# Differential attention: low parts of the queries with zeros on the other 64 partitions

## Chip, cores and metric

The kernel runs on one core of one Trainium2 chip. Times are device microseconds of one execution of the whole program; a change is judged by the median of several executions.

## What is computed

The program is a model of two blocks with two layers each, on 512 tokens of width 1024 (and, in the first block, 256 context tokens). The change touches the differential attention of the first block's second layer alone. It has 8 heads; each has two halves of 64 features, with a softmax of its own each, and one value of 128 features.

```python
def attend(q, k, v):                      # q, k: [2 halves, batch, 8 heads, tokens, 64]
    s = jnp.einsum('cbhqd,cbhkd->cbhqk', q, k).astype(f32)
    p = jax.nn.softmax(s, axis=-1)
    a = p[0] - lam_val * p[1]
    return jnp.einsum('bhqk,bhkv->bhqv', a, v.astype(f32))
...
k_all = jnp.concatenate([kl, kc], axis=3)     # 512 + 256 keys
o_lat = attend over 4 blocks of 128 queries
o = _rmsnorm(o, subln_g) * (1.0 - lambda_init)
```

Queries and keys of the 512 latent tokens are turned by a rotary embedding (rope) first.

## The kernel before

Each product in full precision is made of products of split operands: a number is a high part and a low part, each with at most 12 significant bits, and TensorE adds high x high, low x high and high x low.

Heads are done in four pairs. `project(pr)` (line 1122) is a generator that projects the keys, queries and values of a pair in 12 steps. `ev_q` (line 1127) takes a query head out of PSUM: rope into a scratch tile `qraw` (with a second scratch tile `rot`), then the high part, then the low part. The tile `q` [128, 3, 512] holds three planes. Plane 0 and plane 1 (`cc`) have the high part of half `cc` twice, on its own 64 partitions and on the other 64. Plane 2 has the low parts of both halves, each on its own 64 partitions. `ev_k` (line 1138) does the same for a key head with the scratch `kraw`; its tile `kx` [128, 2, 768] has for half `cc` the high part on its own partitions and the low part on the other ones.

`attend` (line 1171) takes one head, in four blocks `t` of 128 queries. For each half and each 384 of the 768 keys there are two score products into one bank: plane `cc` of `q` against `kx[:, cc]` on all 128 rows (high x high and high x low at once), then plane 2 on the 64 rows of the half against the key's high part:

```python
self.mm(s[cc][:, f, 0:384], q[:, cc, t * P:(t + 1) * P], kx[:, cc, fs], stop=False)
self.mm(s[cc][:, f, 0:384], q[cp, 2, t * P:(t + 1) * P], kx[cp, cc, fs], start=False)
```

So a block has 8 score products and a head 32; the layer has 256. Then VectorE takes the maximum (`nm`, line 1186), ScalarE the exponential (line 1189), VectorE combines the two halves (line 1196), TensorE transposes the result in 4 + 2 pieces through the one bank `a` with a copy by ScalarE after each (line 1203), and multiplies it with the values into bank `o`. After the fourth block `head_norm_out` (line 1227) norms the head in a tile `ho`: a product on VectorE (1232), squares on ScalarE, a power on GpSimd, a second product on VectorE (1240), and four transposes into bank `a`.

The table `da_fill` says how many of the next pair's projection steps go between the blocks of a head: (2, 2, 2, 2, 0) for the first head of a pair and (2, 2, 0, 0, 0) for the second. The last pair has steps of the output projection in their place (`da_last`). A scheduler orders the instructions of each engine from this program when it is built; on the chip each engine takes its instructions in that order. Eight PSUM banks are shared: two for projections (`g`), one `a`, one `o`, two pairs of banks for scores (`s2`). Weights come through SP's DMA queue. `after` (in the first block's program) loads the gate row of the output projection into the tile that was `kraw`, for line 1250.

Of the kernel before, what the change touches and what calls it, by code (L numbers as in the profile page):

```python
# [40 lines left out]
class Kernel:  # L41
    # how many steps of independent work go into the gaps of a chain, ring sizes, scheduling priorities
# [25 lines left out]
    # ---------------------------------------------------------------- helpers  # L68
# [27 lines left out]
    def banks(self, **turns):  # L96
        """a tag takes the banks of these tags in turn (2: halves of s2)"""
        self.turns, self.rest = {k: itertools.cycle(v) for k, v in turns.items()}, None

    def psum(self, **nb):  # L100
        """(re)partition the 8 PSUM banks among tags"""
        if self.pb is not None:
            self.pb.release()
        self.nb = nb
        self.pb = self.pool("ps", 1, PSUM) if nb else None

    def setup(self):
# [17 lines left out]
        self.le = tri("le", -1, 1, ALU.is_ge)   # [p, f] = p <= f  # L125
        self.ge = tri("ge", 1, -1, ALU.is_ge)   # p >= f
        self.gt = tri("gt", 1, -1, ALU.is_gt)   # p > f
        self.lt = tri("lt", -1, 1, ALU.is_gt)   # p < f
# [5 lines left out]
    def open_w(self, raw, hi, unit, side):  # L134
        """rings of weight tiles: raw, high and low parts"""
        return unit, self.pool("wraw", raw, side=side), self.pool("whi", hi, side=side), self.pool("wlo", hi, side=side)
# [8 lines left out]
    def rsqrt(self, out, in_, mul, add, exponent=None):  # L145
        """out = (in_ * mul + add) ** -0.5 on GpSimd, tiny operands"""
# [11 lines left out]
    def exp_ln_tables(self):  # L158
        """the activation tables that hold both exp and ln, from here on"""
        self.tc.keep_in_program_order(self.nc.scalar.preload_act_table_set("natural_log_exp_and_others"))  # L160
# [8 lines left out]
    def rows_to_cols(self, rows, tag, pool=None):  # L169
        """rows: DRAM APs [r, 128] -> const tile [128, sum r], whose columns self.finish_cols() fills"""  # L170
# [18 lines left out]
    def split(self, hi, lo, src, hi_eng):  # L189
        """hi + lo = src exactly, each with at most 12 significant bits"""  # L190
# [3 lines left out]
    def weights(self, src, a, mul=None):  # L194
        """DRAM view [128, a, unit // a] (times mul) -> hi, lo tiles of that shape"""
# [11 lines left out]
    # weights stationary: feature-major result, 256 output features at a time  # L207
# [3 lines left out]
    def gemm_steps(self, w, c0, groups, evac, ncol=256):  # L211
        """groups: lists of segments; a segment is (hi(kt), lo(kt), n). evac(j, [psum per segment])"""
# [12 lines left out]
    def ws_tile(self, ps, wk, j, segs, kts=range(NK)):  # L225
        """128 output features of the segments"""
# [6 lines left out]
    def gemm_halves(self, parts, segs):  # L233
        """the same of several (weights, first column, evac), where the last tokens come late: all products of the
        first segment go ahead"""
# [11 lines left out]
    # tokens stationary: token-major result, 512 output features at a time  # L247
# [14 lines left out]
    def ts_pair_steps(self, wk, hh, hl, t, out):  # L262
        """token tiles t, t + 1, 256 output features each, in the halves of a bank"""
# [16 lines left out]
    # ---------------------------------------------------------------- modulation  # L280
    def ada_setup(self):
# [11 lines left out]
        # column v of s4: vector v; the four column tiles of the array take a k tile each  # L293
# [3 lines left out]
        # sel[r, v]: rows that add up to vector v: v of each column tile, and the bias in row 2; then without the bias  # L297
# [19 lines left out]
    def ada_block(self, l, n, row):  # L317
        """products with columns n * 512 .. of ada_w[l] into row [128, 512], to be summed by sel"""
# [13 lines left out]
    def ada_cols(self, l, sec):  # L332
        """section sec of layer l, feature-major: [128, 8, 2] (lat, ctx)"""
# [13 lines left out]
    def ada_bc_store(self, l, sec, dst):  # L347
        """section sec of layer l to DRAM rows dst [2, 1024] (lat, ctx), to be read back on all partitions"""
# [12 lines left out]
    def load_bc(self, pool, row, tag, n=D):  # L361
        """a DRAM row [n] on all partitions"""
# [4 lines left out]
    # ---------------------------------------------------------------- gated delta net (layer 0)  # L367
# [3 lines left out]
    def load_transposed(self, x_src, ctx_src, xp):  # L371
        """the rows of x and ctx, feature-major: 8 tiles [128, 768]"""
# [21 lines left out]
    def deltanet(self, xp, xT, scratch, zs, gts, later):  # L394
        """normed, gated head outputs before norm_g go to scratch; returns the transposed y"""
# [7 lines left out]
        # shift, scale and the first products, in halves of the features  # L403
# [37 lines left out]
        # decay and beta  # L441
# [52 lines left out]
        def conv_silu2(blk, dst, ps):  # L494
            """dst = 2 silu(conv(x))"""
# [16 lines left out]
        for grp in range(4):  # L512
# [7 lines left out]
            # independent work for the gaps of the chains  # L520
# [26 lines left out]
    def dn_gate(self, half, w, hh, hl, onep, zs):  # L547
        """2 silu(z) of two heads, token-major, to DRAM"""
# [11 lines left out]
    def dn_project(self, grp, w, segs, one, onep, conv_silu2, beta, eg, fill, first):  # L560
# [8 lines left out]
        def sums(src, tag):  # L569
            """sums of squares per token, of twice the value"""  # L570
# [3 lines left out]
            # as rows, two chunks per column tile of the array; then transposed  # L574
# [64 lines left out]
    def dn_tmp(self, one, shape):  # L639
        """one of a ring of 4 KB scratch tiles"""  # L640
# [8 lines left out]
    def dn_prepare(self, p, one, g):  # L649
        """inverses of both directions' triangular systems, and the q k products times the decays: their upper  # L650
        triangle is for direction 0, the lower one for direction 1"""
# [4 lines left out]
        for j, h in enumerate(heads):  # L656
            # decays between tokens j, i: a sum over an empty range in one of the two directions
# [34 lines left out]
    def dn_invert(self, Wt, one):  # L692
        """Wt[:, u] (unit triangular but for its diagonal; u < 12 upper, u >= 12 lower) -> its inverse, in place"""
# [7 lines left out]
        # [(b, i), u, j] -> [(b, u), i, j]: one matrix per partition  # L701
# [17 lines left out]
        # [0]: blocks of the inverse, [1]: their transposes; direction 0 was inverted transposed  # L719
# [8 lines left out]
        # 32 -> 64: source block row, target block row, per direction and pair  # L728
# [23 lines left out]
        # transposed 64-blocks: direction 0 in rows 0:64, direction 1 in rows 64:128  # L752
# [8 lines left out]
        # 64 -> 128  # L761
# [106 lines left out]
    def dn_store(self, p, O, one, scratch):  # L868
        """half the normed head outputs to DRAM"""
# [17 lines left out]
    # ---------------------------------------------------------------- shared pieces  # L887
    def dn_output(self, k, scratch, zs, yh, yl, yp, zp):
        """y = norm(o) * silu(z), transposed and split into yh, yl (norm_g applied on the way)"""
# [16 lines left out]
    def scaled_split(self, hi, lo, ps, scale):  # L906
        """hi + lo = ps * scale"""
# [39 lines left out]
    def proj_steps(self, w, xh, xl, k0, k1, tiles, evac, ncol=512):  # L947
        """token-major projection of k tiles k0 .. k1 of the transposed, split activations by w, in steps;
        evac(t, c0, psum[:, :ncol])"""
# [13 lines left out]
    def ln_stats(self, x, pool):  # L963
        """1 / std and mean per token"""
# [10 lines left out]
    def layernorm(self, x, pool):  # L975
        """x <- (x - mean) * rstd, per token"""
# [6 lines left out]
    def layernorm_affine(self, x, g, b, pool):  # L983
        """x <- (x - mean) * rstd * g + b, per token"""
# [10 lines left out]
    def transpose_split(self, xt, hh, hl, t0, t1, sc, sh, pool, tag="s"):  # L995
        """token tiles xt[t0:t1] -> feature-major hi / lo columns, times sc(k) plus sh(k) per feature"""
# [19 lines left out]
    def fold_cols(self, tag, g, b, sc, sh):  # L1016
        """LN gain and bias folded into the modulation: scale g (1 + sc), bias b (1 + sc) + sh; [128, 8, 2] each"""
# [18 lines left out]
    # gated FFN; gate/up feature-major, down token-major, in chunks of the hidden features  # L1036
    def ffn(self, ntok, emit_hidden, w_down, acc, sb, nring, sizes, add=False, before=None, final=None, mul=None,
            order=None):
        """emit_hidden(pair, hi tiles, lo tiles): two hidden feature tiles. acc[t] (+)= hidden @ w_down, in chunks of
        sizes, w_down times mul; before(): ahead of the last chunk, whose product goes to final(t, c0, psum)"""  # L1040
# [23 lines left out]
        # the down product runs behind the hidden features  # L1064
# [22 lines left out]
    # ---------------------------------------------------------------- differential attention (layer 1)  # L1087
# [1176 lines left out]
```

## Time and profile before

| | |
|---|---|
| median of 3 runs | 3865.22 us |
| lowest, highest | 3863.72, 3866.85 us |
| profiled execution, span of its instructions | 3858.7 us |
| TensorE busy | 3740.8 us, 97% |
| weight loads of TensorE busy | 3033.0 us, 79% |
| VectorE busy | 2343.5 us, 61% |
| ScalarE busy | 1541.7 us, 40% |
| GpSimd busy | 440.1 us, 11% |

The profile is one execution; its page gives the span from the first to the last instruction. In its rows PE is TensorE's matmuls and PEld its weight loads, DVE is VectorE, ACT ScalarE, POOL GpSimd, SP SyncE, and SPq the DMA queue that SP fills. `g<-wh,h3h` names tiles as out<-in: the first input of a matmul is the moving one, the second the stationary one. A matmul's length is its way through the array, so matmuls overlap, and the rate is read from start to start. "issue" is idle time in which the engine waited for nothing that the profile shows.

### The profile page before, as it was taken

To read this page: it belongs to the slowest core of one execution; us is meant where nothing else is said; L and a number is where in the kernel's file an instruction comes from. 1 tells how busy PE (TensorE), PEld (TensorE's weight loads), DVE (VectorE), ACT (ScalarE), POOL (GpSimd) and SP (SyncE) were. 2 spreads that over 40 slices of the span, in tenths; PEclk is the share of its full clock that TensorE was granted. 3 is DMA by queue.
4 is the path that set the end of the run, shared out by engine and by line. 5 is a ranking of instruction groups with operands and counts; after the bars stand their busy time and mean duration, and the time that the engine had idled before them with its cause. 6 is when DMAs were issued, how large, how long until landed. Compare 5 with 4: busy or idle time off the path is not lost.

```text
span 3858.7 us, 57682 instructions
## 1 busy us (share of the span) xinstructions
PE 3740.8 (97%) x23195; PEld 3033.0 (79%) x23195; DVE 2343.5 (61%) x3919; ACT 1541.7 (40%) x2836; POOL 440.1 (11%) x642
## 2 busy tenths in 40 slices
PE   8999999999999999998999999999999999999999
PEld 5675766888888877777888877788887888888887
DVE  3757655653333676677555656656666777556665
ACT  3444443332211244454222456544334655444332
POOL 3112211040000020003000102100000222100000
PEclk9999999999999999999999998999999999999999
DMA  4234234512122211113333213212332223223232
GB/s 166 77 96 132 88 118 126 175 61 66 56 65 66 69 59 33 34 50 91 98 97 91 86 55 106 65 60 88 99 96 86 72 67 106 87 66 93 91 95 82
DMA packets 248974, 329.47 MB, mean 85 GB/s; under 512 B 14408, under 2 KB 194988, under 8 KB 248705
## 3 DMA queue, kind: packets, MB, share of 16 engines
q1 hardware_dynamic: 248000, 325.40, 27.2%
q8 instruction: 182, 2.98, 0.3%
q14 instruction: 88, 0.71, 0.1%
q0 software_dynamic: 704, 0.37, 0.0%
HBM read 318.09 MB, written 7.63 MB: 84 GB/s over the span
## 4 chain that ended last, share of the span: by engine, by line
PE 83%; DVE 6%; ACT 4%; POOL 3%; issue 2%; DMA 1%; SPq 0%; ACTq 0%; POOLq 0%; DVEq 0%
PE g L163 41%; PE a L163 16%; PE o L163 13%; PE s L163 7%; PE i L163 2%; PE s L167 1%; PE a L167 1%; PE p L163 1%; DVE wl L204 1%; DMA araw<-in_ada_w_dram 1%; ACT wh L203 1%; ACT xr L1480 1%; ACT xr L1477 0%; DVE bst L968 0%; PE g L167 0%
## 5 line engine op out<-in xcount | busy, mean ns | idle before, releaser
L204 DVE TENSOR_TENSOR wl<-wr,wh 128x1024 fp32r<-128x1024 f32 (+1 forms) x508 | 587.6, 1164 | 435.8 <-ACT wh L203 420.8
L203 ACT CAST wh<-wr 128x1024 fp32r<-128x1024 f32 (+1 forms) x508 | 493.5, 981 | 783.6 <-PE o L163 373.1
L163 PE MATMUL g<-wh,fh 128*128 128x512 f32 x396 | 156.4, 395 | 0.0
L163 PE MATMUL g<-wh,fl 128*128 128x512 f32 x396 | 156.1, 395 | 0.0
L163 PE MATMUL g<-wl,fh 128*128 128x512 f32 x396 | 155.1, 392 | 0.0
L163 PE MATMUL g<-h2l,wh 128*128 128x512 f32 x352 | 138.0, 392 | 2.4 <-DVE h2l L1014 2.4
L163 PE MATMUL g<-h2h,wh 128*128 128x512 f32 x352 | 137.5, 392 | 0.0
L163 PE MATMUL g<-h2h,wl 128*128 128x512 f32 x352 | 137.1, 390 | 0.0
L163 PE MATMUL a<-araw,s 128*32 128x512 f32 x352 | 125.7, 617 | 6.2 <-DMA araw<-in_ada_w_dram 5.9
L163 PE MATMUL g<-hh,wh 128*128 128x512 f32 (+1 forms) x376 | 115.7, 363 | 1.7 <-ACT hh L421 1.5
L152 POOL TENSOR_SCALAR brs<-bmv 128x1 f32<-128x1 f32 x20 | 9.7, 484 | 932.1 <-DVE bmv L970 922.9
L163 PE MATMUL g<-hh,wl 128*128 128x512 f32 (+1 forms) x376 | 112.6, 358 | 3.5 <-DVE wl L204 3.5
L163 PE MATMUL g<-hl,wh 128*128 128x512 f32 (+1 forms) x376 | 114.0, 358 | 0.8 <-POOL hl L422 0.6
L1049 DVE TENSOR_TENSOR x<-g,x 128x512 f32<-128x512 f32 x120 | 82.5, 688 | 30.5 <-PE g L163 30.3
L163 PE MATMUL s<-k,q 128*128 128x384 f32 (+1 forms) x256 | 98.7, 440 | 0.0
L1186 DVE TENSOR_REDUCE nm<-s 128x1 f32<-128x768 f32 x64 | 61.1, 955 | 52.3 <-PE s L163 52.3
L163 PEld LDWEIGHTS g<-hh,wh 128*128 128x128 f32 x376 | 63.5, 193 | 35.5 <-issue 20.5
L163 PEld LDWEIGHTS g<-hl,wh 128*128 128x128 f32 x376 | 63.4, 192 | 32.6 <-issue 23.7
L163 PEld LDWEIGHTS g<-hh,wl 128*128 128x128 f32 x376 | 62.7, 192 | 32.4 <-issue 21.3
L163 PEld LDWEIGHTS g<-wh,fh 128*128 128x128 f32 x396 | 74.4, 188 | 17.4 <-ACT fh L2096 0.6
L1291 ACT CAST fh<-sg 128x768 fp32r<-128x768 f32 (+1 forms) x44 | 32.0, 726 | 138.9 <-DVE sg L1290 138.9
L163 PEld LDWEIGHTS g<-wl,fh 128*128 128x128 f32 x396 | 74.4, 188 | 16.6
(994 smaller groups left out, 11513.5 us busy)
## 6 DMA issues: line engine op xcount, KB each, us to landing
wr<-in_ffn_w_up_dram SPq DMA_DIRECT2D x132, 512.0 KB, 3.7
araw<-in_ada_w_dram SPq DMA_DIRECT2D x192, 256.0 KB, 3.1
wr<-in_ffn_w_down_dram SPq DMA_DIRECT2D x88, 512.0 KB, 3.7
wr<-in_ffn_w_gate_dram SPq DMA_DIRECT2D x44, 512.0 KB, 3.8
wr<-in_dn_w_in_dram SPq DMA_DIRECT2D x66, 256.0 KB, 2.8
wr<-in_xa_w_kv_dram SPq DMA_DIRECT2D x32, 512.0 KB, 3.9
wr<-in_hgrn_w_in_dram SPq DMA_DIRECT2D x32, 512.0 KB, 4.2
wr<-in_da_w_in_dram SPq DMA_DIRECT2D x24, 512.0 KB, 3.5
```

Of the source, the lines that this page charges most:

```text
L152: nc.gpsimd.tensor_scalar(out=out, in0=in_, scalar1=mul, scalar2=add, op0=MUL, op1=ADD)
L163: self.nc.tensor.matmul(out, lhsT=lhsT, rhs=rhs, start=start, stop=stop)
L167: self.nc.tensor.transpose(out, in_, self.ident[0:k, 0:k])
L203: nc.scalar.copy(hi, raw)
L204: nc.vector.tensor_tensor(out=lo, in0=raw, in1=hi.bitcast(F32), op=SUB)
L1049: nc.vector.tensor_tensor(out=a, in0=ps, in1=a, op=ADD)
L1186: nc.vector.tensor_reduce(out=nm, in_=s[cc][:, :, 0:384], axis=AX.XY, op=MAX, negate=True)
L1291: nc.scalar.copy(hi[j], sg[j])
L1480: nc.scalar.activation(y, x, AF.Copy, scale=rs)
```

## The change

The tile `q` has four planes: plane 2 + `cc` has the low part of half `cc` on its own 64 partitions, and zeros on the other 64, set by GpSimd. The second score product uses plane 2 + `cc` and the key's plane `cc` on all 128 rows. The zeros meet the key's low part, so the sum is as before. To make room, the queries' scratch is the key's `kraw`, and rope's scratch is a tile of the ring `ho` of the head's norm, which has one buffer. Comments and docstrings are dropped too; one line more stands from `ev_q` on, so line numbers are higher by one there, and by two or one behind.

```diff
         def rope(dst, ps):
-            rot = one([P, SEQ], "rot", 1)
+            rot = one([P, NT, P], "ho", 1).rearrange("p t d -> p (t d)")
...
             def ev_q(j, ps):
-                raw = one([P, SEQ], "qraw")
+                raw = kraw[:, 0:SEQ]
                 rope(raw, ps[0])
-                q[j] = one([P, 3, SEQ], "q", 2, F32R)
+                q[j] = one([P, 4, SEQ], "q", 2, F32R)
                 for cc in range(2):
                     own, other = halves[cc], halves[1 - cc]
                     nc.scalar.copy(q[j][own, cc, :], raw[own])
                     (nc.vector, nc.gpsimd)[cc].tensor_copy(q[j][other, cc, :], raw[own])
-                    nc.vector.tensor_tensor(out=q[j][own, 2, :], in0=raw[own], in1=q[j][own, cc, :].bitcast(F32), op=SUB)
+                    nc.gpsimd.memset(q[j][other, 2 + cc, :].bitcast(F32), 0.0)
+                    nc.vector.tensor_tensor(out=q[j][own, 2 + cc, :], in0=raw[own], in1=q[j][own, cc, :].bitcast(F32), op=SUB)
...
                 for cc in range(2):
-                    cp = slice(64 * cc, 64 * cc + 64)
                     for f in range(2):
                         fs = slice(f * 384, (f + 1) * 384)
                         self.mm(s[cc][:, f, 0:384], q[:, cc, t * P:(t + 1) * P], kx[:, cc, fs], stop=False)
-                        self.mm(s[cc][:, f, 0:384], q[cp, 2, t * P:(t + 1) * P], kx[cp, cc, fs], start=False)
+                        self.mm(s[cc][:, f, 0:384], q[:, 2 + cc, t * P:(t + 1) * P], kx[:, cc, fs], start=False)
```

The scheduler's order moves at few places. On TensorE most of the order is the same; at the end of a pair, in the first head of the next one, four transposes (`a<-ident,p`), four scores, two transposes and the product with the values (`o<-v,aT`) stood so before:

```order
L167 MATMUL a_14203<-ident_63,p_14190 128x128 x4
L163 MATMUL s_2673_14219<-k_13273,q_13782 128x384 x4
L167 MATMUL a_14209<-ident_63,p_14190 128x128 x2
L163 MATMUL o_13995<-v_13204,aT_14202 128x128 x6
L163 MATMUL s_2674_14220<-k_13273,q_13782 128x384 x4
```

and in the changed program:

```order
L163 MATMUL s_2669_14223<-k_13275,q_13783 128x384 x4
L163 MATMUL s_2670_14224<-k_13275,q_13783 128x384 x2
L167 MATMUL a_14108<-ident_63,p_14089 128x128 x2
L163 MATMUL o_13999<-v_13206,aT_14101 128x128 x6
L167 MATMUL a_14207<-ident_63,p_14194 128x128 x4
L163 MATMUL s_2670_14224<-k_13275,q_13783 128x384 x2
```

The transposes of one block have moved behind projections, so that two blocks' transposes come close together; between the second block's four transposes and its two stand two scores (and three projections). This is at two pair ends; at all other places four, six or eight scores stand between the transposes as before.

On VectorE, at the same place, the rope of the next pair's key (lines 1117 to 1120) stood ahead of the head's norm (lines 1232 and 1240) before:

```order
L1117 STREAM_SHUFFLE rot_14070<-g_14020 128x512
L1118 TENSOR_TENSOR x_1658_7564<-g_14020,x_1657_7562 128x512
L1119 TENSOR_TENSOR rot_14070<-rot_14070,x_1657_7562 128x512
L1187 TENSOR_SCALAR nm_14087<-nm_14087 128x1
L1195 RECIPROCAL r_2632_13996<-sm_14081 128x1
L1120 TENSOR_TENSOR x_1658_7564<-x_1658_7564,rot_14070 128x512
L1232 TENSOR_TENSOR ho_13946<-o_13623,r_2553_13624 128x512
```

and in the changed program it stands behind it, since its scratch is the same buffer:

```order
L1233 TENSOR_TENSOR ho_13950<-o_13625,r_2551_13626 128x512
L1187 TENSOR_REDUCE nm_14191<-s_2651_14118 128x1
L1241 TENSOR_TENSOR ho_13950<-ho_13950,hms_13952 128x512
L1188 TENSOR_SCALAR nm_14191<-nm_14191 128x1
L1187 TENSOR_REDUCE nm_14196<-s_2652_14119 128x1
L1117 STREAM_SHUFFLE ho_14074<-g_14024 128x512
L1118 TENSOR_TENSOR x_1658_7564<-g_14024,x_1657_7562 128x512
```

The shuffle reads a bank of the projection (`g`) and now writes the buffer that TensorE's transposes of the head read.

On GpSimd, in the second pair's queries, the changed program has the memsets ahead of and behind the cast of the queries, and ahead of the head's power (`hms`):

```order
L1137 MEMSET q_13783 64x512 x2
L152 TENSOR_SCALAR hms_13606<-hms_13606 128x4
L156 TENSOR_TENSOR hms_13606<-hms_13606,mhalf_78 128x4
L1136 CAST q_13783<-x_1658_7564 64x512
L1137 MEMSET q_13822 64x512
L1136 CAST q_13822<-x_1658_7564 64x512
L1137 MEMSET q_13822 64x512
```

Before, the casts and the `hms` rows stood there alone. On SP's queue the load of the gate row (`x<-gts`) has moved behind four other loads.

## Rows read from the trace of the kernel before

**Rows 1.** The page, busy time of each engine, its share of the span and instructions.

```profile
PE 3740.8 (97%) x23195; PEld 3033.0 (79%) x23195; DVE 2343.5 (61%) x3919; ACT 1541.7 (40%) x2836; POOL 440.1 (11%) x642
```

**Rows 2.** The page, the chain that ended last, by engine.

```profile
PE 83%; DVE 6%; ACT 4%; POOL 3%; issue 2%; DMA 1%; SPq 0%; ACTq 0%; POOLq 0%; DVEq 0%
```

**Rows 3.** Stretches: from:to, us, PE, PEld, DVE, ACT, POOL busy, granted clock, DMA, GB/s.

```profile
1412.00:1757.00 345.00, 338.20 (x1925) 269.14 (x1925) 226.89 (x421) 163.02 (x335) 17.77 (x24) 0.99 0.13 40
1499.30:1522.40 23.10, 23.10 (x125) 17.06 (x124) 19.19 (x40) 11.78 (x26) 0.87 (x1) 1.00 0.15 46
...
1673.20:1694.60 21.40, 21.40 (x103) 14.77 (x102) 16.53 (x36) 10.98 (x22) 0.87 (x1) 1.00 0.22 75
1694.60:1740.40 45.80, 43.23 (x201) 30.63 (x199) 31.79 (x64) 23.48 (x56) 2.41 (x4) 0.89 0.08 23
1700.90:1711.10 10.20, 10.20 (x33) 7.16 (x32) 4.96 (x10) 4.07 (x8) 0.00 (x0) 0.50 0.00 0
```

**Rows 4.** Waits of PE from 1412 to 1757: us in total, times, longest us.

```profile
PE a L167 <- DVE ho L1240: 4.2, 4, 1.2
PE a L167 <- DVE rt L1193: 2.6, 1, 2.6
```

**Rows 5.** Timeline of PE at the first scores: start us, us, engine, line, operation.

```profile
1424.51 0.28 PE L163 MATMUL g<-wl,h3h 128*128 128x256 f32 x1
1424.63 2.93 PE L163 MATMUL s<-k,q 128*128 128x384 f32 x8
...
1427.82 0.39 PE L163 MATMUL g<-h3l,wh 128*128 128x512 f32 x1
1428.06 0.40 PE L163 MATMUL g<-h3h,wl 128*128 128x512 f32 x1
1428.29 0.39 PE L163 MATMUL g<-h3h,wh 128*128 128x512 f32 x1
```

**Rows 6.** Timeline of PEld there, with the idle time before in brackets.

```profile
1424.51 0.19 PEld L163 LDWEIGHTS s<-k,q 128*128 128x128 f32 x1
1424.89 0.18 PEld L163 LDWEIGHTS s<-k,q 64*128 64x128 f32 x1 [0.19 <-issue]
```

**Rows 7.** Stretches, instructions with the tile q alone; columns as in rows 3.

```profile
1412.00:1757.00 345.00, 98.68 (x256) 48.45 (x256) 14.39 (x24) 9.88 (x16) 6.55 (x8) 0.99 0.13 40
1499.30:1522.40 23.10, 8.91 (x24) 4.54 (x25) 2.31 (x4) 1.24 (x2) 0.87 (x1) 1.00 0.15 46
...
1673.20:1694.60 21.40, 10.43 (x28) 5.13 (x28) 2.28 (x4) 1.24 (x2) 0.87 (x1) 1.00 0.22 75
1694.60:1740.40 45.80, 22.09 (x52) 10.67 (x52) 0.00 (x0) 0.00 (x0) 0.00 (x0) 0.89 0.08 23
```

**Rows 8.** Timeline, all engines, one block's transposes and their copy.

```profile
1446.65 0.60 PE L167 MATMUL a<-ident,p 128*128 128x128 f32 x4
...
1447.33 0.59 ACT L1203 COPY aT<-a 128x512 f32<-128x512 f32 x1
...
1448.47 0.44 PE L167 MATMUL a<-ident,p 128*128 128x128 f32 x2
```

**Rows 9.** Timeline, all engines, the end of the first pair.

```profile
1520.17 0.36 PE L163 MATMUL g<-h3h,wh 128*128 128x256 f32 x1
...
1524.82 0.69 DVE L1240 TENSOR_TENSOR ho<-ho,hms 128x512 f32<-128x512 f32 x1
...
1526.42 0.60 PE L167 MATMUL a<-ident,ho 128*128 128x128 f32 x4
```

**Rows 10.** Groups by line, GpSimd: xcount | busy us, mean ns | idle.

```profile
L1889 POOL MEMSET keep<- 128x512 f32 x1 | 0.5, 525 | 0.0
```

**Rows 11.** Timeline of VectorE and of SP's queue in the last pair.

```profile
1679.85 50.27 SPq L200 DMA_DIRECT2D wr<-in_da_w_out_dram  x2
1685.96 0.69 DVE L1136 TENSOR_TENSOR q<-qraw,q 64x512 fp32r<-64x512 f32 x1
...
1712.75 0.68 DVE L1250 TENSOR_TENSOR p<-g,x 128x512 f32<-128x512 f32 x1
```

## The prediction

> **What bounds the kernel now.** I read the page's engine lines first: TensorE is busy 97% of the span [rows 1], and the chain that ended last runs through it for 83% [rows 2]. So I looked only at the stage that the change touches. It lies between 1412 and 1757 us, from the first query cast to the last head. There TensorE is busy 338.20 of 345.00 us, at a granted clock of 0.99 (full is 2.4 GHz), VectorE 226.89, ScalarE 163.02, GpSimd 17.77 [rows 3]. TensorE waits for another engine only five times, 6.8 us in all [rows 4]. A microsecond taken out of TensorE's own work there is therefore a microsecond of the kernel, until VectorE and ScalarE can no longer follow.
>
> "Busy" does not say that TensorE goes at its pace. The starts do. A product with 256 moving columns is followed by the next start after 0.12 us (1424.51 to 1424.63) and one with 512 after 0.23 us (1428.06 to 1428.29) [rows 5]. Columns cost the difference, 0.11 us per 256, so one with 384 should take about 0.175. The eight score products from 1424.63 on do not: they and the first product behind them reach to 1427.82, which is 3.19 us [rows 5]. The loads show why. The load for the first score product starts at 1424.51, together with the product before it, so it is hidden. The next, for the 64-row product, starts at 1424.89 only, after 0.19 us of idle with nothing to wait for but "issue" [rows 6]. It starts when its own product starts, so its 0.18 us are exposed. The same holds at each change between 128 and 64 rows, in both directions, and score products alternate strictly.
>
> **What the change does to that.** All 256 score products [rows 7] take 128 rows, so no change of shape is left. Eight of them and the product behind should take 8 x 0.175 + 0.23 = 1.63 us, not 3.19. That is 1.56 us for eight, 0.195 each, and 256 x 0.195 = **50 us off TensorE**. Below this gain I count what is given back.
>
> (a) Transposes have one PSUM bank. Four transposes (start 1446.65) are copied out by ScalarE until 1447.92, and only then can the other two come, at 1448.47 now [rows 8]. Four score products fill the gap. They will take 0.78 us less, the slack is 0.55, so each such place waits some 0.24 us. In the order of the changed program four products stand alone in that gap seven times, and a gap of like length stands there twice more: 9 x 0.24 = 2.2 us back.
>
> (b) Thin stretches. In the second head of each of the first three pairs no projection is left as filling. From 1499.3 to 1522.4 VectorE is busy 19.19 of 23.10 us [rows 3] with 24 score products inside [rows 7]. Taking out 24 x 0.195 = 4.7 would leave 18.4, less than VectorE needs; at most 3.9 can be had, and I take 3.5, for links between VectorE and ScalarE. That is 1.2 back, and the stretch comes three times (the third is 1673.2 to 1694.6, VectorE 16.53 of 21.40, 28 products): 3.6 us.
>
> (c) Ends of a pair. Head output goes through VectorE, ScalarE and GpSimd and is ready at 1525.51, 5.3 us after TensorE turned to other products (1520.17); TensorE asks for it at 1526.42, so 0.9 us are to spare [rows 9]. Eight score products between shrink by 1.56, so 0.65 us becomes a wait, at the ends of the first two pairs: 1.3 us (the third lies in (d)). At the ends of a pair's first head no score product lies between, and the wait there stays.
>
> (d) The last pair has 52 score products after 1694.6 [rows 7], worth 10.1 us. Here TensorE already waits for 2.6 us [rows 4], the eight products ahead of that wait give nothing (1.56), and VectorE is busy 31.79 of 45.80 us [rows 3]. I take 60% as kept: 4 us back. The ends are 1.6 and 8. One thing goes the other way: from 1700.9 to 1711.1 the granted clock is 0.50 (1.2 GHz) [rows 3], so less work for TensorE there is worth a little more; under 1 us, not counted.
>
> Sum: 50 - 2.2 - 3.6 - 1.3 - 4 = **39 us**.
>
> The other edits I cost at nothing, with these covers. *Sixteen memsets on GpSimd*: none of this shape is in the trace. Nearest is a memset of 128x512 with 0.525 us [rows 10]; half the partitions give no reason for more, and under zero it can't go, so 0 to 0.525 each, 8.4 us at most on an engine that works 17.77 of 345. They stand ahead of GpSimd's cast of the queries and ahead of its part of the head's norm. The queries made in one pair are used in the next, and the norm comes after the last score product that frees the tile; if that cover went, (c) would grow by 0.5 us at some five places, 2.6 us. *Rope's scratch in the tile of the head output*: the shuffle now waits on VectorE until TensorE has transposed the head; behind it on VectorE stand the key's rope, a weight split and the next maximum. At the end of a pair the rope moves behind that head's two multiplications. Its key is used in the next pair only and the bank that it empties is asked for one product group later; if that cover goes, about 1 us at each of five head ends, 5 us, within the low end of the range. *Queries in the key's scratch*: no step moves in VectorE's order for it. The load of the gate row into that tile waits for the last query part now (1686.65 today) and is first read at 1712.75; behind it on SP's queue stands one weight load, the second of two that now go out 50 us apart, so it is not held up [rows 11].
>
> Profiled span is 3858.7 us and the median of the runs is 3865.22; 6.5 us lie around the span and are not touched. So 3865.2 - 39 = **3826 us** (span about 3820).
>
> **Rivals.** *TensorE stays the bound everywhere*: (a) to (d) cost nothing, for the chain also starts earlier. For it: VectorE is idle for 118 of the 345 us [rows 3]. Against: the slacks of 0.55 and 0.9 are smaller than what goes away. 50 us, 3815.
>
> *The helpers take half*: the losses of (a) to (d) come out at twice as much, through VectorE, which is at 83% in the thin stretches, and the shared tile of the ropes. For it: each head has the same tight chain of maximum, exponential and combination. Against: outside the stretches of (b) and (d) VectorE is busy only some 140 of 232 us (the row of the first thin stretch taken for the second, too) [rows 3]. Some 25 us are left, 3840.
>
> *No change*: the exposed load is no matter of 64 rows, and full products would expose it too. A load of 0.19 and a stream of 0.175 in turn give 0.365 a product, and 8 of them with the product behind 3.15, near the 3.19 seen now [rows 5], so 3865. Against it stands that the full-height load at 1424.51 does start beside a full-height product [rows 5, 6]. The Trainium skill has a rule that would give just this (TensorE: Matmul & The Clock Gate, Part 3): loads overlap running products only where the row group differs, and two full-height ones share all row groups. By that rule the time stays at 3865; the trace speaks against it, since loads of 0.19 us run beside products that start every 0.12. The skill's page TensorEngine Tiling (Array Packing), Key Properties, speaks for the forecast instead: a change of the tiling mode drains the array.
>
> *Slower*: a faster TensorE idles more and its clock falls. After the wait of 2.6 us the granted clock is 0.50 for 10.2 us [rows 3, 4], which costs 5.1 us. There are 8 head ends and 3 thin stretches; if all 11 brought such a stretch, 56 us would be lost against 50 gained: 3871. [...] The other four waits for a head output share 4.2 us, the longest 1.2, none with a fall of the clock, and I expect 0.65 for the new ones.
>
> **Numbers.** Forecast, 34 to 44 us off: 0.60. Bound stays TensorE: 0.17. Helpers take half: 0.16. No change: 0.04. Slower: 0.03. The range takes in the first three, with 1 to 2 us for what lies round 3815 and 3840: 3813 to 3842. About 0.2%, 8 us, is what a measurement of this kernel can tell. Faster by more 0.93, within 0.04, slower 0.03.
>
> **What would show it.** Right: score products start 0.17 to 0.18 us apart with loads beside them and no idle by "issue"; the stage lasts about 306 us; TensorE's waits for head outputs and for the copy of the transposes rise from 6.8 to some 15 us. Step (a) is wrong if the second transposes come without a wait, (b) if VectorE stays under 85% in the thin stretches, (c) if the head's transposes at a pair's end start with no wait. The whole is wrong if score products still start 0.36 us apart, or if the granted clock is 0.50 in several stretches between 1412 and 1720.

## The result and the profile after

The changed kernel takes **3826.41 us** (median of 4 runs, 3823.06 to 3828.16), the kernel before 3866.03 beside it (4 runs, 3863.72 to 3868.61). The ratio is 0.990, with a 95% interval from 0.9888 to 0.9912. The forecast was 3826. The profiled span is 3821.3 us, 37.4 less than before.

The page's engine line and chain, which answer to [rows 1, 2]:

```profile
PE 3702.9 (97%) x23195; PEld 3032.5 (79%) x23195; DVE 2339.6 (61%) x3919; ACT 1541.2 (40%) x2836; POOL 447.3 (12%) x658
...
PE 82%; DVE 7%; ACT 5%; POOL 3%; issue 2%; DMA 1%; SPq 0%; ACTq 0%; POOLq 0%; DVEq 0%
```

On the page little is to be seen: TensorE is still busy 97%, of a shorter span. The stage tells more. Spans differ by some microseconds from run to run through places that no edit here touches, so from here on **the stage** is measured, from the first score product to the first product of the next layer (`g<-h4h,wh`). The stretches of the kernel before (columns as in [rows 3]):

```profile
1424.63:1781.31 356.68, 348.29 (x1928) 274.34 (x1926) 237.94 (x442) 163.91 (x335) 18.32 (x28) 0.99 0.15 47
```

and of the changed kernel: the stage, its half-clock stretch, the first thin stretch, the end of the first pair, and the third thin stretch.

```profile
1426.90:1745.50 318.60, 305.88 (x1928) 268.89 (x1926) 235.47 (x442) 162.96 (x335) 24.00 (x40) 0.99 0.17 52
...
1671.97:1678.80 6.83, 5.39 (x20) 4.82 (x21) 4.39 (x9) 2.32 (x5) 0.28 (x1) 0.50 0.00 0
1493.83:1513.48 19.65, 19.57 (x125) 16.60 (x124) 16.80 (x35) 11.15 (x25) 1.74 (x3) 1.00 0.17 55
1513.48:1516.99 3.51, 2.63 (x20) 2.45 (x18) 1.80 (x4) 1.15 (x6) 1.20 (x2) 1.00 0.00 0
...
1650.05:1667.46 17.41, 17.35 (x105) 14.24 (x104) 16.47 (x36) 10.80 (x22) 1.74 (x3) 1.00 0.35 122
```

The stage went from 356.68 to 318.60 us, 38.1 less: the whole gain lies there. TensorE does the same number of products in 42.4 us less of busy time (348.29 to 305.88), and its idle time rises from 8.4 to 12.7.

The timeline of PE at the first scores, which answers to [rows 5], and of its loads, to [rows 6]:

```profile
1426.78 0.28 PE L163 MATMUL g<-wl,h3h 128*128 128x256 f32 x1
1426.90 1.55 PE L163 MATMUL s<-k,q 128*128 128x384 f32 x8
1428.29 0.39 PE L163 MATMUL g<-h3h,wh 128*128 128x512 f32 x1
1428.52 0.40 PE L163 MATMUL g<-h3l,wh 128*128 128x512 f32 x1
```

```profile
1426.78 1.35 PEld L163 LDWEIGHTS s<-k,q 128*128 128x128 f32 x8
1428.12 0.19 PEld L163 LDWEIGHTS g<-h3h,wh 128*128 128x128 f32 x1
```

Eight score products take 1.39 us (1426.90 to 1428.29), 0.174 each, and with the product behind them 1.62, where 3.19 stood before and 1.63 was forecast. Each load starts one product ahead of its own, with no idle by "issue". Over the whole stage that idle is gone, and another wait of the loads has come. PEld before, from 1420 to 1780 (us in total, times, longest us), and after it the changed kernel:

```profile
PEld s L163 <- issue: 40.0, 203, 0.3
...
PEld a L167 <- ACT aT L1203: 0.8, 4, 0.2
```

```profile
PEld a L167 <- ACT aT L1204: 8.0, 28, 0.5
...
PEld s L163 <- issue: 1.3, 3, 0.4
```

PE's own waits for the heads, which answer to [rows 4]:

```profile
PE a L167 <- DVE ho L1241: 4.7, 5, 1.3
PE a L167 <- DVE rt L1194: 4.0, 1, 4.0
PE a L167 <- DVE nm L1188: 1.8, 2, 0.9
```

These are the head's transposes again (the releaser `rt` or `nm` is only what VectorE did last): 10.5 us where 6.8 stood.

### The profile page after: what moved, and what is told of

It is laid out like the page before. It is cut to its first block, busy times and chain, and to the rows that moved or that the text cites. A ratio compares the mean times of both kernels' runs of the same rounds, so it can differ in the third digit from the quotient of the medians.

```text
span 3821.3 us, 57711 instructions
## 1 busy us (share of the span) xinstructions
PE 3702.9 (97%) x23195; PEld 3032.5 (79%) x23195; DVE 2339.6 (61%) x3919; ACT 1541.2 (40%) x2836; POOL 447.3 (12%) x658
## 4 chain that ended last, share of the span: by engine, by line
PE 82%; DVE 7%; ACT 5%; POOL 3%; issue 2%; DMA 1%; SPq 0%; ACTq 0%; POOLq 0%; DVEq 0%
PE g L163 41%; PE a L163 16%; PE o L163 13%; PE s L163 6%; PE i L163 2%; PE s L167 1%; PE a L167 1%; DVE wl L204 1%; PE p L163 1%; ACT wh L203 1%; ACT xr L1481 1%; ACT hsq L1238 1%; DMA araw<-in_ada_w_dram 0%; POOL hms L156 0%; ACT xr L1478 0%
## 5 line engine op out<-in xcount | busy, mean ns | idle before, releaser
L163 PEld LDWEIGHTS g<-wh,fl 128*128 128x128 f32 x396 | 74.4, 188 | 16.5 <-DVE fl L2098 0.4
L1291 DVE TENSOR_TENSOR sg<-g,sg 128x512 f32<-128x512 f32 x33 | 22.8, 691 | 98.1 <-PE g L163 98.1
```

The source lines that it names most:

```text
L163: self.nc.tensor.matmul(out, lhsT=lhsT, rhs=rhs, start=start, stop=stop)
L1291: nc.vector.tensor_tensor(out=s, in0=p[:, 0:n], in1=s, op=MUL)
```

## The experiments

All were timed beside the kernel before, which had medians of 3862.52 us beside e1 to e4, 3861.87 beside e5, e6, e8 and e9, and 3862.31 beside e7, e10 and e11; so ratios are to be compared, and not times. For each the stage of its one profiled run is given too, and how much of it ran at a granted clock of 0.50 (1.2 GHz). By estimate half of that time would be won at full clock, so it alone moves the stage by some microseconds.

| kernel | median us | ratio to before (95%) | stage us | of it at 0.50 |
|---|---|---|---|---|
| before | 3866.03 | | 356.7 | 10.2 |
| changed | 3826.41 | 0.990 (0.9888 to 0.9912) | 318.6 | 6.8 |
| e1_64rows | 3861.63 | 1.0001 (0.9992 to 1.0009) | 356.4 | 10.2 |
| e2_two_by_two | 3841.23 | 0.9946 (0.9934 to 0.9959) | 333.9 | 10.2 |
| e3_four_by_four | 3839.97 | 0.9946 (0.9932 to 0.996) | 334.4 | 17.0 |
| e4_own_tiles | 3822.59 | 0.9901 (0.9885 to 0.9916) | 319.6 | 6.8 |
| e5_even_fill | 3820.14 | 0.9895 (0.988 to 0.991) | 318.5 | 3.4 |
| e6_late_head | 3825.75 | 0.991 (0.9895 to 0.9925) | 321.3 | 6.8 |
| e7_three_three | 3822.86 | 0.9892 (0.9875 to 0.9908) | 319.6 | 6.8 |
| e8_own_tiles_even | 3822.86 | 0.9899 (0.9883 to 0.9916) | 317.1 | 0 |
| e9_both | 3815.93 | 0.9885 (0.9871 to 0.99) | 312.2 | 0 |
| e10_last_filled | 3822.56 | 0.9893 (0.9879 to 0.9908) | 320.8 | 6.8 |
| e11_both_three | 3817.61 | 0.9883 (0.9868 to 0.9897) | 313.7 | 0 |

### Only the rows undone

Run e1_64rows. The changed kernel, with the second product on its own 64 rows again; tiles, zeros, scratches and memsets stay.

```diff
-self.mm(s[cc][:, f, 0:384], q[:, 2 + cc, t * P:(t + 1) * P], kx[:, cc, fs], start=False)
+self.mm(s[cc][:, f, 0:384], q[64 * cc:64 * cc + 64, 2 + cc, t * P:(t + 1) * P], kx[64 * cc:64 * cc + 64, cc, fs], start=False)
```

> All edits of the change stay (four planes with zeros, the shared scratch tiles, the memsets), but the second score product takes the 64 rows of its half again. Theory (the exposed load at each change between 128 and 64 rows is the whole gain, the other edits cost nothing): 3866 us, within 0.2% of the kernel before. Rival (the other edits move the time too): 5 us or more away from it, slower if the shared tiles or the memsets cost, faster if the moved rope gives something.

Measured 3861.63 us, 0.9 below its own base of 3862.52, ratio 1.0001. The waits of the loads are those of before:

```profile
PEld s L163 <- issue: 39.9, 203, 0.3
```

So the rows are the whole effect, and the other edits together cost nothing that can be measured (some 0.1%).

### Half as many changes of shape

Run e2_two_by_two. The kernel before, with the four products of a half in the order 128, 128, 64, 64 rows.

```diff
 for f in range(2):
     fs = slice(f * 384, (f + 1) * 384)
     self.mm(s[cc][:, f, 0:384], q[:, cc, t * P:(t + 1) * P], kx[:, cc, fs], stop=False)
+for f in range(2):
+    fs = slice(f * 384, (f + 1) * 384)
     self.mm(s[cc][:, f, 0:384], q[cp, 2, t * P:(t + 1) * P], kx[cp, cc, fs], start=False)
```

> The kernel before with the order of the score products changed alone: for each half both 128-row products, then both 64-row ones, so 4 changes of the row count per block of 8 instead of 8. Theory (each change exposes 0.195 us): 128 changes less, 25 us off TensorE, some 80% of it kept, 3846 us. Rival (a 64-row load is never hidden, whatever stands before it, and the 128-row load behind one neither): 3 of 4 loads stay exposed, 12 us off TensorE, 3856 us. Rival (alternation plays no part, 64 rows are slow as such): 3866 us.

Measured 3841.23 us, 21 below its own base of 3862.52; the stage is 22.8 shorter. Counted in TensorE's order of the trace there are 132 changes of rows where 256 were: 124 x 0.195 = 24.2. Loads of this kernel at the first scores:

```profile
1427.27 0.31 PEld L163 LDWEIGHTS s<-k,q 128*128 128x128 f32 x2
1427.83 0.29 PEld L163 LDWEIGHTS s<-k,q 64*128 64x128 f32 x2 [0.25 <-issue]
1428.38 0.30 PEld L163 LDWEIGHTS s<-k,q 128*128 128x128 f32 x2 [0.25 <-issue]
1428.92 0.29 PEld L163 LDWEIGHTS s<-k,q 64*128 64x128 f32 x2 [0.25 <-issue]
```

The second load of two like ones is beside the first product; the idle stands at the changes alone. So it is the change that costs, not the 64 rows and not the full height.

### A quarter of the changes

Run e3_four_by_four. All four 128-row products of a block, then its four 64-row products, the halves in turn.

```diff
 for cc in range(2):
-    cp = slice(64 * cc, 64 * cc + 64)
     for f in range(2):
         fs = slice(f * 384, (f + 1) * 384)
         self.mm(s[cc][:, f, 0:384], q[:, cc, t * P:(t + 1) * P], kx[:, cc, fs], stop=False)
+for f in range(2):
+    fs = slice(f * 384, (f + 1) * 384)
+    for cc in range(2):
+        cp = slice(64 * cc, 64 * cc + 64)
         self.mm(s[cc][:, f, 0:384], q[cp, 2, t * P:(t + 1) * P], kx[cp, cc, fs], start=False)
```

> The kernel before with the four 128-row products of a block first and then the four 64-row ones, the halves in turn, so 2 changes per block instead of 8. Theory: 192 changes less, 37 us off TensorE, some 80% kept, 3836 us; if the 64-row products of the two halves, which lie on different rows, run beside each other, up to 11 us more, 3827 us. Rival (64-row loads never hidden): 5 of 8 loads stay exposed, 19 us off TensorE, 3851 us. The later end of the first half's scores delays its maximum, which may cost up to 5 us in the stretches without filling.

A miss: 3839.97 us, no better than two by two. Where eight scores stand together it does what was meant. PE and its loads at the first scores:

```profile
1425.43 1.41 PE L163 MATMUL s<-k,q 128*128 128x384 f32 x8
1426.77 0.50 PE L163 MATMUL g<-h3h,wh 128*128 128x512 f32 x1
```

```profile
1425.31 0.66 PEld L163 LDWEIGHTS s<-k,q 128*128 128x128 f32 x4
1426.22 0.30 PEld L163 LDWEIGHTS s<-k,q 64*128 64x128 f32 x4 [0.25 <-issue]
```

Eight take 1.34 us, a little less than the 1.39 of the changed kernel. But elsewhere the scheduler splits the eight again, half by half, with projections between: the trace has 114 changes, not 64. That gives 142 x 0.195 = 27.7. The stage is 22.3 shorter, with 17.0 us at half clock where 10.2 were, which is 3.4 of time; 22.3 + 3.4 = 25.7. The count of the changes was wrong. Nor is the run a close test of their price: 31 pairs of 64-row products start less than 0.03 us apart in this trace, by estimate worth 0.17 us each (0.70 us for four in turn, less 0.55 - 0.195 for four in pairs, is 0.35 for two pairs), 5 us in all. So 33 were to be had, and where the other 7 went is not shown.

### The same rows without zeros, memsets or shared tiles

Run e4_own_tiles. The kernel before with its own tiles; the plane of both low parts on all 128 rows.

```diff
-self.mm(s[cc][:, f, 0:384], q[cp, 2, t * P:(t + 1) * P], kx[cp, cc, fs], start=False)
+self.mm(s[cc][:, f, 0:384], q[:, 2, t * P:(t + 1) * P], kx[:, cc, fs], start=False)
```

> The kernel before (own scratch tiles for the queries and for rope, three planes, no memsets), but the second score product takes plane 2 with the low parts of both halves on all 128 rows against the key's plane; this adds the product of the other half's low query part with the key's low part to each score. Theory (128 rows give the whole gain, the shared tiles and the memsets cost nothing): as the change, 3826 us, within 3 us. Rival (the shared tile of the ropes or the memsets cost up to 1 us at five head ends): 3821 us or less.

Measured 3822.59 us, which is under the 3826 expected as its base is 3.5 under that of the changed kernel; the ratio of 0.9901 is that of the change, and the stages differ by 1 us. With the first experiment this shows from both sides that memsets and shared tiles are covered, to within what can be measured.

### More filling in the thin stretches

Run e5_even_fill. The changed kernel with another table; the steps are as many, and those of the second head are taken from the first.

```diff
-da_fill = ((2, 2, 2, 2, 0), (2, 2, 0, 0, 0))
+da_fill = ((2, 2, 1, 1, 0), (2, 2, 1, 1, 0))
```

> The changed kernel with the projection steps spread evenly over the heads: da_fill is (2, 2, 1, 1, 0) for both heads of a pair, so the second head's later blocks have filling and more projections stand ahead of the transposes of a head. Theory (what the change did not give is lost in the thin stretches, some 1.2 us each of three, and in waits for the head's norm, 1.4 us at three first heads and 1.05 at two pair ends): up to 3.6 + 4.2 + 2.1 = 10 us come back against the changed kernel, 3816 us; if the queries of the next pair, now projected last, come 2 us late at two pair changes, 3820. Rival (the loss is in the copies of the transposes and in the banks of the scores, wherever the filling stands): the same as the changed kernel, 3824 to 3828 us. Against the kernel before the ratio is then 0.987 to 0.989 by the theory, 0.990 by the rival.

Measured 3820.14 us, ratio 0.9895; its interval, 0.988 to 0.991, holds the ratios of theory and rival alike. The stage decides: it is 318.5, as long as without, though 3.4 us less of it ran at half clock, by estimate 1.7 us of time. So there is no gain. PE's waits in the stage:

```profile
PE a L167 <- DVE ho L1241: 8.8, 8, 1.5
PE s L163 <- ACT p L1190: 2.4, 3, 1.7
```

The long wait in the last pair is gone, but all eight heads still make TensorE wait (1.6 us at the ends of the first two pairs, where 1.05 stood), and the exponentials take 2.4. By the stage the rival came out: what the thin stretches lose does not come back with filling moved there from the first heads.

### The head's transposes later

Run e6_late_head. On the variant with own tiles: the four transposes of a head are written behind the first block of the next head.

```diff
+                if t == 0 and late:
+                    late.pop()()
                 p, sm = [], one([P, 2], "sm", 3)
...
-            self.head_norm_out(po, NT, yh[h], yl[h], gcol, one, scale=r0, tag="a")
+            last = self.head_norm_out(po, NT, yh[h], yl[h], gcol, one, scale=r0, tag="a", defer=True)
+            if h == 7:
+                last()
+            else:
+                late.append(last)
...
```

With `defer`, `head_norm_out` returns its last step, the transposes, as a function to be called later.

> The variant of before with its own tiles and 128-row second products (measured 3822.6 us), with the four transposes of a head written behind the first block's scores and projections of the next head. TensorE's order then has 47 projections between the last product of a first head and its transposes where 27 stood, and 7 more products at a pair's end; in the last pair the order stays. Theory (these waits are losses of their own): three waits of 1.38 us and two of 0.8 go, 5.7 us, 3817 us; the wait of 4.2 us in the last pair stays. Rival (the softmax chain of the next block is as late, and the wait only moves to the next transposes): 3821 to 3825 us. Second rival (the head's buffer is freed later, so the next norm is held up): over 3826 us.

Measured 3825.75 us, stage 321.3, 1.7 longer than without. PE's waits, from 1420 to 1735:

```profile
PE a L167 <- DVE rt L1194: 4.0, 1, 4.0
PE a L167 <- DVE ho L1245: 3.8, 4, 1.4
PE a L167 <- DVE ayl L910: 3.0, 3, 1.0
PE s L163 <- ACT p L1190: 2.8, 6, 0.7
```

The three first heads' waits are gone, and three new ones of 1 us stand in their place: the next block's transposes wait until VectorE has emptied bank `a` of the head (`ayl`). At the two pair ends the wait has grown, from 0.65 to 1.4. So the waits only moved; 3825.75 lies between the ranges of the two rivals.

### Both, on own tiles

Run e8_own_tiles_even is the even table alone on own tiles, run e9_both the same with the late transposes.

> The variant with own tiles and 128-row second products with the even filling (2, 2, 1, 1, 0) for both heads. Theory: the same gain as the even filling brings the changed kernel, so 3813 to 3818 us against 3822.6 without it. Rival (no gain by filling): 3821 to 3825 us. If it gains and the changed kernel with the same filling does not, the shared tile of rope and head norm is what holds that one.

> Own tiles, 128-row second products, even filling and late transposes of a head together. Theory (losses at the thin stretches and at the head ends add up, and each edit takes away its own): the even filling has already most of the waits for a head covered, so 1 to 3 us better than the even filling alone, 3811 to 3816 us. Rival (both edits fill the same gap, or the queries projected last become the new wait): no better than the better of the two alone, 3816 to 3820 us.

The table alone: 3822.86 us. Its stage is 2.5 shorter than without it, and the half clock that is not there is by estimate worth 3.4, so again no gain. Both: 3815.93 us, stage 312.2. Against own tiles alone the stage is 7.4 shorter; 3.4 of that are by estimate the half clock, and 4.0 the two edits. PE's waits in its stage:

```profile
PE a L167 <- ACT aT L1204: 1.7, 3, 0.7
...
PE s L163 <- ACT p L1190: 1.1, 3, 0.5
PE a L167 <- DVE ayl L910: 1.0, 2, 0.5
PE a L167 <- DVE r L1196: 1.0, 1, 1.0
...
PE a L167 <- DVE ho L1245: 0.5, 2, 0.3
```

The waits for a head, 10.5 us in the changed kernel, are down to 1.5 (`ho`, and one listed under `r`), and the bank is waited for 1.0: in TensorE's order 47 or 48 projections now stand ahead of the transposes of the first five heads. The time of 3815.93 lies where the ranges of theory and rival meet. Against the rival it is 7 us better than either edit alone, and the theory's reason did not come out either: each edit alone only moved waits, and together they took most of them away. It is the fastest version here.

### Three and three transposes

Run e7_three_three is the changed kernel, run e11_both_three the fastest version (e9), each with the transposes of a block in 3 + 3 pieces.

```diff
-for c0, c1 in ((0, 4), (4, 6)):
+for c0, c1 in ((0, 3), (3, 6)):
```

> The changed kernel with the transposes of a block in 3 + 3 pieces through bank a, in place of 4 + 2. The measure is the stage from the first score product to the first product of the next layer: 356.7 us before, 318.6 in the changed kernel. Step (a) says that the second transposes wait for the copy of the first (0.59 us for 512 columns) because four full-height score products no longer fill it. With 384 columns in the first copy, and one transpose of 0.11 us moved behind it, the wait of 0.07 to 0.19 us at some 15 places should go: 1.5 to 3 us, stage 315.5 to 317. Rival (the longer second copy makes the product with the values wait as much as is won): 318 to 320. Second rival (the wait is not for the copy but for the array or the combination): second transposes wait as before, 318.6.

> The best version so far (own tiles, 128-row second products, even filling, late transposes of a head; 3815.9 us, stage 312.2) with the transposes in 3 + 3 pieces. If the split gains in the changed kernel it should gain here at the same places: stage 309 to 311, about 3813 us. If the second copy takes it back: 312 to 313.5.

Measured 3822.86 us with a stage of 319.6, and 3817.61 with 313.7: 1.0 and 1.5 us longer. PEld's waits with three and three in the changed kernel:

```profile
PEld a L167 <- ACT aT L1204: 6.5, 27, 0.4
PEld o L163 <- ACT aT L1204: 2.2, 6, 0.4
```

The second transposes wait less (6.5 for 8.0 us), which shows that step (a) waits for the copy; but the product with the values now waits for the longer second copy (2.2, where 1.0 stood). The two together are 8.7 for 9.0 us; what makes the stage 1.0 longer beyond that is not shown. The first rival came out; with both edits the stage is 0.2 over its range.

### Filling for the longest wait

Run e10_last_filled. The changed kernel, with one step of the output projection moved ahead of the sixth head's transposes.

```diff
-da_last = ((0, 0, 0, 1, 0), (0, 2, 1, 1, 3))
+da_last = ((1, 0, 0, 0, 0), (0, 2, 1, 1, 3))
```

> The changed kernel with one step of the output projection moved from the fourth to the first block of the last pair's first head: da_last is ((1, 0, 0, 0, 0), (0, 2, 1, 1, 3)). In TensorE's order 12 projections now stand among the eight score products ahead of the transposes of the sixth head. Step (d): the wait of 4.17 us there is the largest single loss that the change leaves; TensorE has nothing else to do. Theory: 12 products of 0.23, 2.8 us, come out of that wait, and the filling that is missing at the end of the seventh head costs about 1: stage 316 to 317.5 against 318.6. Rival (the last pair is bound by its chain of maximum, exponential and combination, so filling only moves): 318 to 319.5. If the half-clock stretch behind the wait goes too, 3 us more: 313.

Measured 3822.56 us, stage 320.8, 2.2 longer than in the changed kernel; the half-clock stretch stayed. PE's waits in the last pair and behind it, from 1664 to 1748:

```profile
PE s L167 <- ACT x L981: 1.3, 2, 0.9
PE a L167 <- DVE nm L1188: 1.3, 2, 0.8
PE a L167 <- DVE ho L1241: 1.2, 1, 1.2
PE a L167 <- DVE k L910: 1.2, 1, 1.2
PE s L163 <- ACT p L1190: 0.9, 2, 0.5
```

Of the wait of 4 us 0.85 is left, and five kinds of short ones, 5.9 us in all, stand in this list, up to the next layer's inputs. The rival came out and a bit worse: work put into one gap is missing in the next. That fits a last pair bound by its chain through VectorE and ScalarE, which is not shown beyond that.

## Why the prediction was right

**The 50 us off TensorE.** Right, in mechanism and size. Scores start 0.174 us apart (forecast 0.175), and 38.7 of the 40.0 us that loads of scores stood idle are gone. At two other counts the price per change held, though not exactly: 24.2 us worked out against 22.8 measured for 124 changes, and for 142 changes 27.7, with some 5 for products in pairs, against 25.7. "No change" is refuted: full-height loads run beside full-height products. By the rule in the Trainium skill (TensorE: Matmul & The Clock Gate, Part 3) that loads overlap only where the row group differs they should not, and here the measurement decides. The Trainium skill's page TensorEngine Tiling (Array Packing), Key Properties, which has the array drain at a change of mode, agrees with the idle of 0.25 us at each change in the two-by-two order.

**What was given back.** 256 x 0.195 = 49.9. The stage got 38.1 shorter, and by estimate 1.7 of that is 3.4 us less at half clock. So 13.5 us were lost, where the text had 11.1. In the prediction's bounds the stage of 345.0 us became 306.9 (345.0 - 38.1; forecast about 306). TensorE's waits for heads rose from 6.8 to 10.5 us; those for the copies are nearly all too short for PE's list and stand in that of its loads, 8.0. Together that is 18.5, where some 15 was forecast. That the time came out within 0.5 us of 3826 is in part luck: 2.4 us more were lost than the sum had, the clock gave 1.7 back, and the runs of the changed kernel lie 5 us apart.

(a) Where four scores stand alone the mechanism was right; the term was too small, since other places wait as well. The block that was quoted [rows 8] now reads so in the timeline:

```profile
1446.30 0.60 PE L167 MATMUL a<-ident,p 128*128 128x128 f32 x4
...
1446.65 0.94 PE L163 MATMUL s<-k,q 128*128 128x384 f32 x4
1446.98 0.59 ACT L1204 COPY aT<-a 128x512 f32<-128x512 f32 x1
...
1447.62 0.44 PE L167 MATMUL a<-ident,p 128*128 128x128 f32 x2
```

Four scores of 0.174 end at 1447.35, and the transposes come at 1447.62, after the copy: 0.27 (forecast 0.24). But loads wait for the copy at 28 places (the waits of PEld above), 15 of them in the stretches of (b) and (d). The other 13 add up to 3.9 us, and 3.9 is also what (b) to (d) as below leave of the 13.5; the term had 2.2. At four of the 13 four scores stand alone, at two it is two scores and three projections. At the other seven, 2.2 us together, it is eight scores, three times alone and four times with projections, and such places the prediction had not counted. There the copy itself comes late, since ScalarE has other work ahead of it, for example in the second head:

```profile
1478.88 1.05 ACT L203 CAST wh<-wr 128x1024 fp32r<-128x1024 f32 x1 [0.39 <-PE g L163]
...
1480.09 0.59 ACT L1204 COPY aT<-a 128x512 f32<-128x512 f32 x1
...
1480.73 0.20 PEld L167 LDWEIGHTS a<-ident,p 128*128 128x128 f32 x2 [0.26 <-ACT aT L1204]
```

The first transposes there start at 1478.80 and end at 1479.40, the copy starts 0.7 later, and eight scores from 1479.15 on last until 1480.54.

(b) Right in size: 23.10 us [rows 3] became 19.65, so 3.45 were kept (forecast 3.5); the third went from 21.40 to 17.41, 4.0 kept of 5.5. Some 3.9 for all three, against 3.6. The reason fits the third alone, where VectorE is busy 16.47 of 17.41 us, 95%. In the first it is busy 16.80 of 19.65, 85% and just above the sign that was set for this step, where the forecast (19.19 of 19.6) meant 98: 2.4 us of its work have moved out of the stretch, and filling moved there gained nothing. PE has no listed wait in it; its loads wait 0.8 us for copies and 0.7 for exponentials, and which of them sets the pace is open.

(c) Right, and a bit small. The end of the first pair:

```profile
1515.82 0.28 PE L163 MATMUL g<-wl,h3h 128*128 128x256 f32 x1
1516.14 0.69 DVE L1241 TENSOR_TENSOR ho<-ho,hms 128x512 f32<-128x512 f32 x1 [0.81 <-POOL hms L156]
...
1516.99 0.63 PE L167 MATMUL a<-ident,ho 128*128 128x128 f32 x4 [0.88 <-DVE nm L1188]
```

The last product before the transposes starts at 1515.82 and is followed 0.12 later if nothing waits; 1516.99 is 1.05 late, where 0.65 was forecast. The stretch from the eight scores to the head's transposes went from 4.02 us (1522.40 to 1526.42) [rows 9] to 3.51. On own tiles the wait listed there is 0.64 where 0.88 is listed here, so a quarter of a microsecond may come with VectorE's moved order, which the prediction had as covered. At the ends of first heads the wait stayed as forecast, 1.2 us.

(d) Right: the eight products ahead of the long wait gave nothing (1667.46 to 1673.13 is 5.67 us, before 1694.64 to 1700.21, 5.57), as the text had it. TensorE waits that much longer:

```profile
1673.13 0.88 PE L167 MATMUL a<-ident,ho 128*128 128x128 f32 x3 [4.01 <-DVE rt L1194]
```

The 44 behind it are worth 8.6 us and brought 8.4 up to the last head's transposes, of which by estimate 1.7 is the shorter half-clock stretch [rows 3]; so 1.7 + 1.9 = 3.6 were lost, forecast 4. That the clock would give something back was named, and left out of the sum.

**The other edits.** Costed at nothing, and but for the quarter of a microsecond in (c) nothing was measured. The memsets in the stage take 0.521 us each, within the estimate of 0 to 0.525:

```profile
L1137 POOL MEMSET q<- 64x512 f32 x14 | 7.3, 521 | 111.4 <-PE s L163 111.1
```

They wait long, for the scores that free their tile, and nothing asks for them before the next pair. The shared tile holds the next key's rope behind the head; the stage is no longer than with own tiles (318.6 and 319.6).

**The rivals.** "TensorE stays the bound everywhere" (3815) would have needed all of (a) to (d) at nothing; the version with both edits comes near it, 45.9 us under its own base, in part by its clock. "The helpers take half" (3840) put the same losses at twice the forecast's, 22 us, where 13.5 were measured. "Slower" by the clock fell: the one half-clock stretch got shorter, 6.8 for 10.2 us, and no wait but the longest, of 4.0, has one with it. Nor is a long wait what such a stretch needs: with a step of projection moved into that wait (e10) the longest wait left there is 0.85 us, and the stretch of 6.8 us stays; with both edits (e9) waits of up to 1.0 stand there, and none comes. What decides is open.

## What to carry to other kernels

Where products of different row counts alternate, look for idle of the weight loads with nothing to wait for: here each change of rows cost 0.195 us. Giving all of them the same rows, with zeros or with an operand that the other half may meet, cost TensorE nothing here: 128-row products of 384 columns start 0.174 us apart, between the 0.12 at 256 columns and the 0.23 at 512. Count what such a gain meets next: about a quarter of it went to waits that had a slack smaller than what was taken away, and edits that fill one such gap mostly open the next.

## What was not expected of the hardware

Two 64-row products on different halves of the rows run at the same time, which was expected of run e3 only as a possibility. In the four-by-four order their four loads take 0.30 us together, as long as two on the same rows in the two-by-two order (0.29), and their starts in the trace come in pairs 3 ns apart. Four of them need 0.55 us with the change behind them (1426.22 to 1426.77), four 128-row products 0.70. So a group of eight with both its changes takes 1.34 us against 1.39: the halves in parallel just pay for the two changes, as long as nothing splits the group.
